# First stage of a hybrid decoder block: wide shift products, a tied TensorE order, later low parts, and the query banks emptied first

## Chip, core and metric

The kernel runs on one core of one Trainium2 chip. The metric is the device time of one execution in microseconds, as the median of several runs. The engines are TensorE (PE in the profile, its weight loads PEld), VectorE (DVE), ScalarE (ACT), GpSimd (POOL) and SyncE (SP, which issues loads).

## What is computed

One decoder layer on a sequence of 1024 positions with 1024 channels: a token-mixing part (a convolution branch and a stick-breaking attention branch, merged by gates) and a SwiGLU part, each between two RMS norms, with shift, scale and gate from a conditioning vector `c`. The change touches the start:

```python
c_act = jax.nn.silu(c)
mod = c_act @ ada_w[l] + ada_b[l]
sh1, sc1, ga1, sh2, sc2, ga2 = [m[:, None, :] for m in jnp.split(mod, 6, axis=-1)]
h = rmsnorm(x, pre_mix_g[l]) * (1.0 + sc1) + sh1
proj = h @ w_in        # gives GLU inputs, q, k, v and two merge gates
```

## The kernel before

Channels lie on the 128 partitions, so the 1024 channels are eight tiles (`KT` = 8, index k) of 128 x 1024; positions are the free dimension, in two halves of 512 (`NCH` = 2, index c). Products are made from float32r values split in two: a high part (`hhi`, `w0hi`) and a low part (`hlo`, `w0lo`, the rest). A product of h with a weight is three sums: high x high, low weight x high h, high weight x low h.

The first stage does this:

- Loads, all issued by SP (L98): `vec`, the eight tiles of `xT`, then the eight pieces of the modulation weight (`ada_w`, 1 MB each: shift half and scale half, in five buffers) with three weights (`w0raw`) between the first ones. These weights are those of the first query, the first key and the first GLU gate tile (`pq0`, `pk0`, `pgg0`, two PSUM banks each).
- The squares of x (ACT, L247) are summed over the channels on PE (L250) with a matrix of ones, and `rstd` is made from the sums (L327 to L338).
- For each k the scale is a dot product on DVE (`dots`, L121). The shift is, for k = 0 to 4, a product on PE (`shift_pe`, L280: eight one-column products, each two instructions, into column k of `psh`) and an addition on ACT (`shift_act`, L284); for k = 5 to 7 it is a second dot product on DVE.
- `x_op` (DVE, L296) multiplies x by scale and rstd in place; `hi_op` (ACT, L299) adds the shift and rounds to `hhi`; `lo_op` (DVE, L302) makes `hlo`. `w0_hi` (ACT, L307) and `w0_lo` (DVE, L311) split the three weights. POOL issues the stores of x (L101).
- `gemm_k` (L317) adds the k-th contribution to the three pairs of banks. Tile 0 is taken in halves; steps 0 and 1 serve the weights that are split by then.

Then `qk_pair(0)` empties the query banks (ACT L499 and L500, DVE L501 and L502) and the key banks (ACT L510 to L513, DVE L516), and `v_half(0)` makes the value tiles (L478): its two weights are loaded and split (`load_w`, L145 on ACT and L155 on DVE) into the slots that the first stage's weights had, its tiles go through the three banks of the pool `psm`, which the query and key banks held, and are evacuated by L482 (ACT) and L483 (DVE). Behind that come the GLU (`glu`), the attention (`attend`, z at L548 and L549) and everything else.

A planner writes the order of each engine's instructions when the kernel is built, from priorities and modelled durations. `pin` ties the instructions of the named engines to the order of the program. Before the change, DVE and ACT are tied in the first stage and PE is not; `qk_pair(0)` is not tied. The planner also adds the waits between engines.

Of the kernel before, what the change touches and what calls it, by code (L numbers as in the profile page):

```python
# [10 lines left out]
F32 = mybir.dt.float32  # L11
F32R = mybir.dt.float32r
AF = mybir.ActivationFunctionType
ALU = mybir.AluOpType
# [3 lines left out]
P = 128  # L18
D = 1024
T = 1024  # L20
KT = D // P
# [14 lines left out]
SH_DVE = (5, 6, 7)  # L36
# [24 lines left out]
C_ADAB = 32  # L61
# [8 lines left out]
def tile_block(ctx: ExitStack, tc: tile.TileContext, xT, vecs, ada1, ada2, win, wv, wcv, wat, wo, w1, w2, cvw, out):  # L70
    nc = tc.nc
    act, dve, pool, pe = nc.scalar, nc.vector, nc.gpsimd, nc.tensor
# [30 lines left out]
    vec = small.tile([P, NVEC], F32, name="vec")  # L103
# [4 lines left out]
    ones = small.tile([P, P], F32, name="ones")  # L108
# [60 lines left out]
    PINNED = tuple(getattr(mybir.EngineType, e) for e in ("PE", "DVE", "Activation"))  # L169
    START_PIN = PINNED[1:]  # L170

    def pin(start, engines=PINNED):
        last = {}
        for i in nc.cur_bb.bb.instructions[start:]:
            if i.engine not in engines:
                continue
            if i.engine in last:
                tc.add_manual_dep(i, last[i.engine].name,
                                  mybir.DependencyInfo(mybir.DependencyClass.NoSync, mybir.DependencyReason.SCHED_ONLY))
            last[i.engine] = i  # L180
# [16 lines left out]
    with ExitStack() as s0:  # L197
# [11 lines left out]
            load(aws[k], ada1[k])  # L209

        pvar = [ps0.tile([P, CH], F32, tag="pvar", name=f"pvar{c}", bufs=2) for c in range(NCH)]
        psh = ps0.tile([P, KT], F32, name="psh")
        rstd = p0.tile([P, T], F32, name="rstd0")
        csil = small.tile([P, KT], F32, name="csil")
        sc1 = small.tile([P, KT], F32, name="sc1")
# [36 lines left out]
        for k in range(KT - 1):  # L252
            if k == 0:
                square(0, rstd)
                continue
            sq = sq_tile0(f"sq{k}")
            square(k, sq)
            if k % 2:
                for c in range(NCH):
                    sums(sq, c, first=k == 1)  # L260
            elif k < KT - 2:
                dve.tensor_tensor(rstd, rstd, sq, op=ALU.add)
            else:
                for c in range(NCH):
                    dve.tensor_tensor(rstd[:, hs[c]], rstd[:, hs[c]], sq[:, hs[c]], op=ALU.add)
# [9 lines left out]
        def shift_of(k):  # L275
            return mod[:, k:k + 1]

        def shift_pe(k):
            for kt in range(KT):
                pe.matmul(psh[:, k:k + 1], aws[k][:, 0, kt * P:(kt + 1) * P], csil[:, kt:kt + 1],  # L280
                          start=(kt == 0), stop=(kt == KT - 1))

        def shift_act(k):
            act.activation(shift_of(k), psh[:, k:k + 1], AF.Identity, bias=vec[:, C_ADAB + k:C_ADAB + k + 1], scale=1.0)  # L284

        def dots(k):
            if k in SH_DVE:
# [10 lines left out]
        def hi_op(k, cols=slice(0, T)):  # L298
            act.activation(hhi[k][:, cols], xs[k][:, cols], AF.Identity, bias=shift_of(k), scale=1.0)  # L299
# [10 lines left out]
        def w0_lo(i):  # L310
            dve.tensor_tensor(w0s[i][1], w0raw[i], w0s[i][0], op=ALU.subtract)  # L311

        def gemm_k(b_, w, k):
            cols = slice(k * P, (k + 1) * P)
            for q, (st, mv) in enumerate(((0, 0), (0, 1), (1, 0))):
                for c, bank_ in b_.items():
                    pe.matmul(bank_, w[st][:, cols], h[mv][k][:, hs[c]], start=(k == 0 and q == 0),  # L317
                              stop=(k == KT - 1 and q == 2))

        for k in range(KT):  # L320
            hhi.append(hp.tile([P, T], F32R, tag="act", name=f"hhi{k}"))
            hlo.append(hp.tile([P, T], F32R, tag="act", name=f"hlo{k}"))

        shift_pe(0)
        for c in range(NCH):
            r, (m, a) = rstd[:, hs[c]], rt[c]
# [7 lines left out]
        for c in range(NCH):  # L334
            r, (m, a) = rstd[:, hs[c]], rt[c]
            dve.tensor_tensor(a, r, r, op=ALU.mult)
            dve.scalar_tensor_tensor(a, m, -0.5, a, op0=ALU.mult, op1=ALU.mult)
            dve.scalar_tensor_tensor(r, a, 1.5, r, op0=ALU.add, op1=ALU.mult)  # L338
            x_op(0, hs[c])
            hi_op(0, hs[c])  # L340
        dots(1)
        w0_lo(0)
        lo_op(0)
        for k in range(KT):
            kn = k + 1
            if kn < KT:
                if kn not in SH_DVE:
                    shift_act(kn)
                if kn + 1 < KT and kn + 1 not in SH_DVE:
                    shift_pe(kn + 1)  # L350
                x_op(kn)
                if kn <= 2:
                    w0_hi(kn)
                hi_op(kn)
                if kn + 1 < KT:
                    dots(kn + 1)
                if kn <= 2:
                    w0_lo(kn)
            if k:
                lo_op(k)  # L360
            store(xm_d[k], xs[k])
            ws = (q0b, k0b, gg0b)
            if k <= 1:
                for i in range(k + 1):
                    gemm_k(ws[i], w0s[i], k)
                for kk in range(k + 1):
                    gemm_k(ws[k + 1], w0s[k + 1], kk)
            else:
                for b_, w_ in zip(ws, w0s):
                    gemm_k(b_, w_, k)  # L370
        high.__exit__(None, None, None)
        pin(begin, START_PIN)
        sg0 = []
        for c in range(NCH):
            sg = sgp.tile([P, CH], F32, tag="sg", name=f"sg0_{c}", bufs=2)
# [29 lines left out]
    with ExitStack() as sC:  # L405
        pc = mkpool(sC, "pc")
        with ExitStack() as sA:
# [55 lines left out]
                                       scale=1.0)  # L463
                    load(u_d[ct][hf * (NG // 2):(hf + 1) * (NG // 2)].rearrange("g p m -> p g m"), o)

            def v_half(hf):
                w = [load_w(wv[hf, g], f"wv{hf}_{g}", act, pool if hf else dve) for g in range(2)]
                tiles = []
                for tb in range(KT):
                    if tb % 2 == 0:  # L470
                        vslot = pa.tile([P, 2, 4, 2, HD], F32R, tag="vst", name=f"vst{hf}_{tb}", bufs=4)
                    pv = bank(f"pv{hf}_{tb}")
                    tcols = slice(tb * P, (tb + 1) * P)
                    for k in range(KT):
                        whi, wlo = w[k // 4]
                        wc = slice((k % 4) * 256, (k % 4) * 256 + 256)
                        for i, (st, mv) in enumerate(((hhi, whi), (hlo, whi), (hhi, wlo))):
                            pe.matmul(pv[:, :256], st[k][:, tcols], mv[:, wc],  # L478
                                      start=(k == 0 and i == 0), stop=(k == KT - 1 and i == 2))
                    vt = vslot[:, tb % 2]  # L480
                    pvh = pv[:, :256].rearrange("p (h d) -> p h d", d=HD)
                    act.activation(vt[:, :, 0, :], pvh, AF.Copy)  # L482
                    dve.tensor_tensor(vt[:, :, 1, :], pvh, vt[:, :, 0, :], op=ALU.subtract)  # L483
                    tiles.append(vt)
                return tiles

            def qk_pair(p):
                qs = [pc.tile([P, T], F32R, tag="qst", name=f"qst{p}_{i}", bufs=3) for i in range(2)]
                ks = [pc.tile([P, T], F32R, tag="kst", name=f"kst{p}_{i}", bufs=3) for i in range(2)]
                kl = [pc.tile([P, T], F32R, tag="klo", name=f"klo{p}_{i}", bufs=3) for i in range(2)]  # L490
                A, B = slice(0, HD), slice(HD, P)
                if p == 0:
                    b = q0b
                else:
                    b = banks2(f"pq{p}")
                    gemm(b, load_w(win[8 + p], f"wq{p}"), h, range(KT))
                for c in range(NCH):
                    cs = slice(c * CH, (c + 1) * CH)
                    act.activation(qs[0][A, cs], b[c][A], AF.Copy)  # L499
                    act.activation(qs[1][B, cs], b[c][B], AF.Copy)  # L500
                    dve.tensor_tensor(qs[0][B, cs], b[c][A], qs[0][A, cs], op=ALU.subtract)  # L501
                    dve.tensor_tensor(qs[1][A, cs], b[c][B], qs[1][B, cs], op=ALU.subtract)  # L502
                if p == 0:
                    b = k0b
                else:
                    b = banks2(f"pk{p}")
                    gemm(b, load_w(win[12 + p], f"wk{p}"), h, range(KT))
                for c in range(NCH):
                    cs = slice(c * CH, (c + 1) * CH)
                    act.activation(ks[0][A, cs], b[c][A], AF.Copy)  # L510
                    act.activation(ks[1][B, cs], b[c][B], AF.Copy)
                    act.activation(ks[0][B, cs], b[c][A], AF.Copy)
                    act.activation(ks[1][A, cs], b[c][B], AF.Copy)  # L513
                    for i, src in enumerate((A, B)):
                        for dst in (A, B):
                            dve.tensor_tensor(kl[i][dst, cs], b[c][src], ks[i][src, cs], op=ALU.subtract)  # L516
                return qs, ks, kl
# [86 lines left out]
                return nxt  # L604

            with tc.high_priority(offset=SOONER):
                qk = qk_pair(0)
            v = v_half(0)
            for p in range(4):
                glu(p)  # L610
                if p == 2:
# [1223 lines left out]
```

## Time and profile before

| | us |
|---|---|
| median of 3 runs | 1400.02 (1399.16 to 1400.69) |
| profiled execution | 1400.8 |
| its span, first to last instruction | 1399.0 |
| first stage, up to the first value product | 68.1 |

The profile is one execution. A timeline row gives start, duration, engine, line, operation, output and inputs, tile and count; in brackets stands how long the engine was idle before and what ended that. Several instructions in one row have the duration from the first start to the last end. Matmuls are pipelined and their ends are modelled, so the pace of a sequence is read from the starts or from the chain of waits.

### The profile page before, as it was taken

Reading aid. Unit: us, or ns where it says so; the run is one execution under the profiler, and the core shown is the slowest. Engines: PE = TensorE matmul, PEld = TensorE weight load, DVE = VectorE, ACT = ScalarE, POOL = GpSimd, SP = SyncE. Lnnn points to the kernel's source line nnn. Section 1 sums busy time; section 2 is a strip of 40 time slices with the busy share of each in tenths; the row PEclk is TensorE's granted clock in tenths of the full one; section 3 lists DMA queues with packets and bytes.
Section 4 is the critical chain, followed back from the end, with each engine's and each line's share of the span. In section 5 each row is a group of like instructions: output and inputs, shape, how many; then the busy total and the mean of one; then the engine's idle time right before and its main releaser. Section 6 shows DMA issues by size and latency. Waiting matters only on the chain.

```text
span 1399.0 us, 18714 instructions
## 1 busy us (share of the span) xinstructions
PE 1370.6 (98%) x6778; PEld 1150.3 (82%) x6778; DVE 1043.6 (75%) x1592; ACT 651.5 (47%) x1147; POOL 109.4 (8%) x251
## 2 busy tenths in 40 slices
PE   8999999999999999999999999999999999999996
PEld 5898898998987887888887778888888887888886
DVE  7898586775858789677597887778887876785355
ACT  6375465464546456213366553334454444433441
POOL 0100000000000011000012100001111110000002
PEclk8999999999999999999999999999999999999999
DMA  9512050141359646855845635457777779586736
GB/s 384 204 31 76 31 166 31 61 121 46 123 191 318 203 128 233 308 183 176 311 136 188 196 115 192 142 179 249 252 241 263 248 240 398 176 330 229 249 110 121
DMA packets 94684, 265.01 MB, mean 189 GB/s; under 512 B 10048, under 2 KB 21440, under 8 KB 93568
## 3 DMA queue, kind: packets, MB, share of 16 engines
q1 hardware_dynamic: 74352, 201.68, 43.2%
q0 software_dynamic: 18224, 58.47, 11.9%
q10 hardware_dynamic: 2016, 3.67, 0.7%
q8 instruction: 53, 0.87, 0.3%
q14 instruction: 39, 0.32, 0.1%
HBM read 192.74 MB, written 71.04 MB: 189 GB/s over the span
## 4 chain that ended last, share of the span: by engine, by line
PE 76%; issue 14%; DVE 3%; DMA 3%; ACT 2%; POOL 1%; POOLq 0%; DVEq 0%; SPq 0%; ACTq 0%
PE ka L1001 14%; PE ka L1543 9%; PE kc L1001 8%; PE pwo L919 5%; PE pb L1543 4%; PE pgv L166 3%; PE pyc L747 3%; PE pya L166 3%; PE pv L478 3%; PE pq L166 2%; PE pk L166 2%; PE pgg L166 2%; PE pa L1543 2%; PE kb L1001 2%; PE tr L574 2%
## 5 line engine op out<-in xcount | busy, mean ns | idle before, releaser
L550 ACT ACTIVATE ka<-z 128x128 f32<-128x128 f32 (+2 forms) x96 | 47.4, 496 | 53.0 <-PE z L549 43.7
L556 DVE TENSOR_TENSOR_SCAN ka<-ka,eye 128x128 f32<-128x128 f32 (+1 forms) x64 | 51.9, 824 | 17.1 <-ACT ka L550 17.1
L1543 PE MATMUL ka<-gt,w2f 128*128 128x512 f32 x264 | 63.4, 389 | 0.0
L121 DVE SCALAR_TENSOR_TENSOR ada<-ada,cb 128x1024 f32<-128x1024 f32 x32 | 39.0, 1223 | 27.5 <-DMA ada<-in_ada_dram 27.5
L1543 PEld LDWEIGHTS ka<-gt,w2f 128*128 128x128 f32 x264 | 49.6, 188 | 10.3
L561 DVE TENSOR_TENSOR be<-be,ka 128x127 f32<-128x127 f32 (+2 forms) x96 | 52.0, 553 | 7.2 <-ACT be L552 1.8
L1109 PE MATMUL ke<-b,w_hi 128*128 128x512 f32 x176 | 55.2, 395 | 0.0
L552 ACT ACTIVATE be<-z 128x127 f32<-128x127 f32 (+2 forms) x96 | 47.0, 496 | 3.9 <-PE tr L574 3.8
L574 PE MATMUL tr<-ident,be 128*128 128x128 f32 x288 | 47.3, 272 | 0.0
L559 DVE TENSOR_TENSOR_SCAN ka<-ka 128x512 f32<-128x512 f32 x32 | 40.4, 1274 | 4.3 <-ACT ka L550 4.2
L458 PE MATMUL pcv<-ph,cvw 128*128 128x128 f32 x320 | 43.1, 274 | 0.0
L458 PEld LDWEIGHTS pcv<-ph,cvw 128*128 128x128 f32 x320 | 40.6, 191 | 0.7
L1109 PEld LDWEIGHTS ke<-b,w_hi 128*128 128x128 f32 x176 | 32.9, 188 | 7.9 <-issue 0.7
L580 ACT ACTIVATE ahi<-tr 128x512 fp32r<-128x512 f32 x48 | 28.3, 600 | 23.1 <-PE tr L574 17.4
L145 ACT ACTIVATE gt<-X 128x512 fp32r<-128x512 f32 x33 | 20.3, 629 | 39.6 <-DVE X L1586 17.5
L581 DVE TENSOR_TENSOR alo<-tr,ahi 128x512 fp32r<-128x512 f32 x48 | 32.3, 684 | 8.5 <-ACT ahi L580 8.3
L478 PE MATMUL pv<-wv_hi,hhi 128*128 128x256 f32 x128 | 36.7, 287 | 1.6 <-DVE vst L483 0.9
L145 ACT ACTIVATE s1o<-s 128x512 fp32r<-128x512 f32 x22 | 13.8, 629 | 50.4 <-PE ka L1001 44.0
L574 PEld LDWEIGHTS tr<-ident,be 128*128 128x128 f32 x288 | 34.8, 140 | 2.8
L402 PE MATMUL k<-hhi,a 128*128 128x512 f32 x112 | 35.4, 391 | 1.7 <-ACT ee L635 1.6
L478 PE MATMUL pv<-wv_hi,hlo 128*128 128x256 f32 x128 | 36.7, 287 | 0.0
L478 PE MATMUL pv<-wv_lo,hhi 128*128 128x256 f32 x128 | 36.3, 285 | 0.0
(550 smaller groups left out, 4178.6 us busy)
## 6 DMA issues: line engine op xcount, KB each, us to landing
w_d<-w2o POOLq DMA_DIRECT2D x44, 512.0 KB, 7.5
w2f<-w_d SPq DMA_DIRECT2D x44, 512.0 KB, 4.3
ada<-in_ada_dram SPq DMA_DIRECT2D x32, 512.0 KB, 5.1
w2r<-in_w_dram SPq DMA_DIRECT2D x44, 256.0 KB, 3.8
w1g<-in_w_dram SPq DMA_DIRECT2D x21, 512.0 KB, 3.7
w1u<-in_w_dram SPq DMA_DIRECT2D x21, 512.0 KB, 5.7
cvw<-in_cvw_dram SPq DMA_DIRECT2D x20, 512.0 KB, 3.7
ada_w<-in_ada_dram SPq DMA_DIRECT2D x8, 1024.0 KB, 14.0
```

The lines of the kernel that those rows point to most:

```text
L166: pe.matmul(bank, st[:, cols], mv[k][:, c * CH:(c + 1) * CH], start=(i == 0 and s == 0), stop=(i == n - 1 and s == 2))
L458: pe.matmul(cv[:, gi * TM:(gi + 1) * TM], wts[n][:, at:at + P], ph[:, g, SH - 1 - d:SH - 1 - d + TM], start=(d == 0), stop=(d == SH - 1))
L478: pe.matmul(pv[:, :256], st[k][:, tcols], mv[:, wc], start=(k == 0 and i == 0), stop=(k == KT - 1 and i == 2))
L550: act.activation(kap[:, s_lo:s_hi], z[:, zo:zo + w], AF.Sigmoid, bias=0.0, scale=-0.125)
L552: act.activation(beta[:, :m], z[:, zo:zo + m], AF.Sigmoid, bias=0.0, scale=0.125)
L556: dve.tensor_tensor_scan(rev, rev, eye[:, CH - w:][:, ::-1], 0.0, op0=ALU.mult, op1=ALU.add)
L561: dve.tensor_tensor(beta[:, :m], beta[:, :m], kap[:, s_lo + 1:s_lo + 1 + m], op=ALU.mult)
L574: pe.transpose(tr[:, o:o + P], probs[ii][:, jo:jo + P], ident)
L919: pe.matmul(bank_, st[:, cols], mv[k][:, cs], start=(k == 0 and q == 0), stop=(k == KT - 1 and q == 2))
L1001: pe.matmul(bank_, st[:, cols], t[:, mv], start=(first and j == 0 and s == 0), stop=(j == HK - 1 and s == 2), skip_group_check=not first)
L1109: pe.matmul(kbs[f], wes[f][st][:, cols], t[:, mv], start=(i == 0 and j == 0 and q == 0), stop=(j == HK - 1 and q == 2), skip_group_check=i ...
L1543: pe.matmul(dst, w[st][:, cols], g[mv], start=first and s == 0, stop=last and s == 2, skip_group_check=more)
```

## The change

The scalars of `c` are copied over 128 equal columns (`csb`, made by DVE in the middle of the squares), and a shift is a product with 128 moving columns into one of four slots of `psh`, of which ACT reads the first column. `shift_pe` for tile 2 goes between the two halves of tile 0, and the later ones stand one step further ahead. `gemm_k` becomes `gemm_q`, which takes the list of part products (HH, HL, LH: weight part, then h part): a step makes HH and LH of its own tile and HL of the tile before, and the last step makes both HL, one weight after the other. PE is tied to the program's order from the first shift to the end of the stage. `qk_pair` takes a function that it calls after each query half; for the first pair this loads and splits a value weight, and DVE and ACT are tied there.

```diff
-    def pin(start, engines=PINNED):
+    def pin(start, engines=PINNED, end=None):
         last = {}
-        for i in nc.cur_bb.bb.instructions[start:]:
+        for i in nc.cur_bb.bb.instructions[start:end]:
...
-        psh = ps0.tile([P, KT], F32, name="psh")
+        psh = ps0.tile([P, 4, P], F32, name="psh")
+        csb = p0.tile([P, KT, P], F32, name="csb")
...
             elif k < KT - 2:
                 dve.tensor_tensor(rstd, rstd, sq, op=ALU.add)
+                if k == 2:
+                    for kt in range(KT):
+                        dve.tensor_scalar(csb[:, kt], ones, csil[:, kt:kt + 1], None, op0=ALU.mult)
...
         def shift_pe(k):
             for kt in range(KT):
-                pe.matmul(psh[:, k:k + 1], aws[k][:, 0, kt * P:(kt + 1) * P], csil[:, kt:kt + 1],
+                pe.matmul(psh[:, k % 4], aws[k][:, 0, kt * P:(kt + 1) * P], csb[:, kt],
                           start=(kt == 0), stop=(kt == KT - 1))
 
         def shift_act(k):
-            act.activation(shift_of(k), psh[:, k:k + 1], AF.Identity, bias=vec[:, C_ADAB + k:C_ADAB + k + 1], scale=1.0)
+            act.activation(shift_of(k), psh[:, k % 4, 0:1], AF.Identity, bias=vec[:, C_ADAB + k:C_ADAB + k + 1], scale=1.0)
...
-        def gemm_k(b_, w, k):
+        def gemm_q(b_, w, k, *sms, cs=(0, 1)):
             cols = slice(k * P, (k + 1) * P)
-            for q, (st, mv) in enumerate(((0, 0), (0, 1), (1, 0))):
-                for c, bank_ in b_.items():
-                    pe.matmul(bank_, w[st][:, cols], h[mv][k][:, hs[c]], start=(k == 0 and q == 0),
-                              stop=(k == KT - 1 and q == 2))
+            for st, mv in sms:
+                for c in cs:
+                    pe.matmul(b_[c], w[st][:, cols], h[mv][k][:, hs[c]], start=(k == 0 and st == 0 and mv == 0),
+                              stop=(k == KT - 1 and mv == 1))
+
+        HH, HL, LH = (0, 0), (0, 1), (1, 0)
...
+        pe_begin = len(nc.cur_bb.bb.instructions)
         shift_pe(0)
...
             x_op(0, hs[c])
             hi_op(0, hs[c])
+            gemm_q(q0b, w0s[0], 0, HH, cs=(c,))
+            if c == 0:
+                shift_pe(2)
...
-                if kn + 1 < KT and kn + 1 not in SH_DVE:
-                    shift_pe(kn + 1)
+                if kn + 2 < KT and kn + 2 not in SH_DVE:
+                    shift_pe(kn + 2)
...
-            ws = (q0b, k0b, gg0b)
-            if k <= 1:
-                for i in range(k + 1):
-                    gemm_k(ws[i], w0s[i], k)
-                for kk in range(k + 1):
-                    gemm_k(ws[k + 1], w0s[k + 1], kk)
+            ws = list(zip((q0b, k0b, gg0b), w0s))
+            if k == 0:
+                gemm_q(*ws[0], 0, LH, HL)
+                gemm_q(*ws[1], 0, HH, HL)
+            elif k == 1:
+                gemm_q(*ws[0], 1, HH, LH)
+                gemm_q(*ws[1], 0, LH)
+                gemm_q(*ws[1], 1, HH, LH)
+                gemm_q(*ws[2], 0, HH, HL)
+                gemm_q(*ws[2], 1, HH)
             else:
-                for b_, w_ in zip(ws, w0s):
-                    gemm_k(b_, w_, k)
+                for i, bw in enumerate(ws):
+                    if k == 2 and i == 2:
+                        gemm_q(*bw, 0, LH)
+                        gemm_q(*bw, 1, LH)
+                    gemm_q(*bw, k, HH, LH)
+                    if k == KT - 1:
+                        gemm_q(*bw, k - 1, HL)
+                        gemm_q(*bw, k, HL)
+                if k < KT - 1:
+                    for bw in ws:
+                        gemm_q(*bw, k - 1, HL)
         high.__exit__(None, None, None)
         pin(begin, START_PIN)
+        pin(pe_begin, PINNED[:1])
...
-            def v_half(hf):
-                w = [load_w(wv[hf, g], f"wv{hf}_{g}", act, pool if hf else dve) for g in range(2)]
+            def v_half(hf, w=None):
+                if w is None:
+                    w = [load_w(wv[hf, g], f"wv{hf}_{g}", act, pool if hf else dve) for g in range(2)]
...
+                    if between:
+                        between(c)
...
             with tc.high_priority(offset=SOONER):
-                qk = qk_pair(0)
-            v = v_half(0)
+                begin = len(nc.cur_bb.bb.instructions)
+                wv0 = []
+                qk = qk_pair(0, lambda c: wv0.append(load_w(wv[0, c], f"wv0_{c}", act, dve)))
+                pin(begin, START_PIN)
+            v = v_half(0, wv0)
```

More of the change, by code (lines that the diff above doesn't have):

```diff
@@ L485, in v_half, with qk_pair @@
                 return tiles
-            def qk_pair(p):
+            def qk_pair(p, between=None):
                 qs = [pc.tile([P, T], F32R, tag="qst", name=f"qst{p}_{i}", bufs=3) for i in range(2)]
```

## The prediction

> **What bounds the kernel now.** The page's head and busy shares come first: the end is set by TensorE (PE).
>
> ```profile
> span 1399.0 us, 18714 instructions
> ...
> PE 1370.6 (98%) x6778; PEld 1150.3 (82%) x6778; DVE 1043.6 (75%) x1592; ACT 651.5 (47%) x1147; POOL 109.4 (8%) x251
> ```
>
> Next come the views by windows, since the change touches the first 80 us only (columns: window, its length, busy time and count for PE, PEld, DVE, ACT and POOL, then granted clock, DMA share, GB/s).
>
> ```profile
> 16.87:20.28 3.41, 3.41 (x21) 2.44 (x19) 3.23 (x6) 2.53 (x4) 0.00 (x0) 1.00 1.01 416
> ...
> 23.00:24.00 1.00, 0.00 (x0) 0.00 (x0) 0.96 (x2) 0.00 (x0) 0.00 (x0) 0.85 0.90 365
> ...
> 33.00:34.00 1.00, 1.00 (x6) 0.91 (x5) 0.96 (x3) 1.00 (x1) 0.53 (x1) 0.53 0.95 393
> ...
> 36.00:67.00 31.00, 31.00 (x146) 25.84 (x145) 24.83 (x36) 8.77 (x10) 4.61 (x17) 1.00 0.49 200
> ...
> 67.00:79.00 12.00, 10.37 (x82) 9.70 (x81) 11.22 (x17) 11.43 (x21) 0.00 (x0) 1.00 0.30 88
> ...
> 79.00:200.00 121.00, 120.95 (x757) 108.26 (x756) 96.34 (x144) 67.92 (x145) 2.70 (x27) 1.00 0.21 66
> ```
>
> The granted clock falls from 1.0 to 0.5 in the window from 23 us (0.85 as a mean puts the fall near 23.7) and comes back near 33.9: 10.2 us at half speed. From 36 us on PE has no gap until 67, then loses 1.63 us of 12, then runs full. So what the stage loses, it loses before 34 and between 67 and 79. The PE timeline shows the first place:
>
> ```profile
> 17.65 1.02 PE L250 MATMUL pvar<-sq,ones 128*128 128x512 f32 x2
> ...
> 18.51 1.84 PE L280 MATMUL psh<-csil,ada_w 128*128 128x1 f32 x16
> ...
> 20.71 1.93 PE L280 MATMUL psh<-csil,ada_w 128*128 128x1 f32 x16 [0.36 <-ACT mod L284]
> ...
> 24.95 0.79 PE L317 MATMUL pq<-hhi,w0hi 128*128 128x512 f32 x1 [1.97 <-ACT hhi L299]
> ...
> 25.54 3.41 PE L280 MATMUL psh<-csil,ada_w 128*128 128x1 f32 x16
> ```
>
> Up to 18.5 PE is full with wide products (the sums). Two shift columns (one-column products), a single wide product and a gap of 1.97 us follow, and in them the clock falls; the third shift column then takes 3.41 us. The chain of waits gives the wide product's two rates:
>
> ```profile
> 30.01 1.71 PE pq L317 x4
> ...
> 60.54 0.91 PE pq L317 x4
> ```
>
> That is 0.43 us each at half clock and 0.2275 at full. The end of the stage, from the timelines:
>
> ```profile
> 64.21 1.06 ACT L145 ACTIVATE wv_hi<-wv_raw 128x1024 fp32r<-128x1024 f32 x1 [6.12 <-PE pq L317]
> ...
> 66.73 0.61 PE L317 MATMUL pgg<-hhi,w0lo 128*128 128x512 f32 x2
> ...
> 68.11 0.36 PE L478 MATMUL pv<-wv_hi,hhi 128*128 128x256 f32 x1 [0.77 <-DVE qst L502]
> ...
> 78.53 0.39 PE L478 MATMUL pv<-wv_hi,hhi 128*128 128x256 f32 x1 [0.86 <-DVE vst L483]
> ```
>
> The query products are done at 64.21 (the value weights wait for their slot), the gate products, 12 more, at 64.21 + 12 x 0.2275 = 66.95; the first value product waits for DVE to empty the query bank, the fourth value tile for DVE to evacuate the first.
>
> **The change part by part.** *Wider shift columns.* Each shift is 16 instructions still, with 128 moving columns in place of one. The trace has that shape and type in the convolution, and DVE has the shape of the new 128-column copies of the scalars:
>
> ```profile
> L458 PE MATMUL pcv<-ph,cvw 128*128 128x128 f32 x320 | 43.1, 274 | 0.0
> ...
> 3.22 1.66 DVE L240 TENSOR_SCALAR dia<-ident,csil 128x128 f32<-128x128 f32 x8
> ...
> 11.64 1.23 DVE L262 TENSOR_TENSOR rstd<-rstd,sq 128x1024 f32<-128x1024 f32 x1 [1.39 <-ACT sq L247]
> ...
> 14.22 1.29 DVE L265 TENSOR_TENSOR rstd<-rstd,sq 128x512 f32<-128x512 f32 x2 [1.35 <-ACT sq L247]
> ```
>
> 43.1/320 = 0.135 us, so 2.16 us a shift against 1.84 to 1.93. The bounds are 1.84 (columns cost nothing) and 3.41 (the dearest shift above); I take 2.16, from the same shape at full clock. Five shifts cost PE 1.4 us more. The eight copies cost DVE 1.66 us and stand ahead of the L262 of 11.64: 1.39 lies in its idle time, 0.27 moves it, and the next DVE instruction, which idles 1.35, swallows that. Without this cover it would be 1.66 on DVE.
>
> *TensorE's order tied, low parts a step behind.* PE now runs in program order, each shift further ahead, so it waits for the shift weights' loads. Their issue and time to landing (the DMA view, one issue to an answer; the fourth and fifth lie in the row of four, the fifth at 14.3):
>
> ```profile
> 10.49 0.33 SPq L98 DMA_DIRECT2D ada_w<-in_ada_dram  x1
> ...
> 13.05 12.64 SPq L98 DMA_DIRECT2D ada_w<-in_ada_dram  x4
> ...
> ada_w<-in_ada_dram SPq DMA_DIRECT2D x1, 1024.0 KB, 13.9
> ...
> ada_w<-in_ada_dram SPq DMA_DIRECT2D x1, 1024.0 KB, 15.1
> ...
> ada_w<-in_ada_dram SPq DMA_DIRECT2D x1, 1024.0 KB, 17.2
> ```
>
> They land at 24.4, 28.15 and 31.5. PE then goes: shift 0 from 18.51 to 20.8; ACT's 0.3 us; shift 1 to 23.3; first query product to 23.5; wait to 24.4; shift 2 to 26.6; second product to 26.8; wait to 28.15; shift 3 to 30.3. Behind each waiting shift stand PE's own products. Of the others, ACT's addition for shift 1 may wait until shift 2 is done at 26.6, as all shifts lie in one PSUM tile; behind it on ACT stands the key weight's high part, then done by 28, and DVE takes that at 30.38 (below). The load that reuses shift 0's buffer is issued 0.4 later, behind loads queued up to 31.5. Eight wide products (4 query, 4 key) take 1.8, to 32.1; shift 4 (landed) 2.2, to 34.3. There remain 16, 22 and 4 x 18 products for steps 1 to 6, and 24 for step 7, the query's 8 first. At 0.2275 the query group ends 118 products on: 34.3 + 26.8 = **61.1**, where it now ends at 64.21. Gate products end 16 later, at 64.8, against 66.95 now. This takes full clock throughout: no PE gap is over 1.4 us, and in every stretch of 3.4 us some 60% holds products of 128 columns or more.
>
> Nothing they need is late: DVE and ACT keep their order.
>
> ```profile
> 26.59 1.28 DVE L302 SCALAR_TENSOR_TENSOR hlo<-x,mod,hhi 128x1024 fp32r<-128x1024 f32 x1
> ...
> 30.38 1.22 DVE L311 TENSOR_TENSOR w0lo<-w0raw,w0hi 128x1024 fp32r<-128x1024 f32 x1
> ...
> 56.81 2.59 DVE L302 SCALAR_TENSOR_TENSOR hlo<-x,mod,hhi 128x1024 fp32r<-128x1024 f32 x2
> ...
> 56.93 1.16 ACT L299 ACTIVATE hhi<-x,mod 128x1024 fp32r<-128x1024 f32 x1 [3.98 <-DVE x L296]
> ```
>
> The first low part is there at 27.9 and used after 30.3; the last high part at 58.1 and the last low part at 59.4, used from 59.3 and 60.6 on. The last two leave at most 1.2 us for a faster PE: what is late next is DVE.
>
> The clock is the term to weigh. [...]
>
> *Query evacuation ahead.* ACT and DVE do the same pieces, the first query half before the first value weight.
>
> ```profile
> 65.17 0.57 ACT L499 ACTIVATE qst<-pq 64x512 fp32r<-64x512 f32 x1
> ...
> 66.56 0.68 DVE L501 TENSOR_TENSOR qst<-pq,qst 64x512 fp32r<-64x512 f32 x1
> ...
> 71.14 5.62 DVE L516 TENSOR_TENSOR klo<-pk,kst 64x512 fp32r<-64x512 f32 x8 [0.50 <-ACT kst L513]
> ...
> 76.80 1.23 DVE L155 TENSOR_TENSOR wgv_lo<-wgv_raw,wgv_hi 128x1024 fp32r<-128x1024 f32 x1
> ...
> 78.05 1.09 DVE L483 TENSOR_TENSOR vst<-pv,vst 128x256 fp32r<-128x256 f32 x3
> ```
>
> After the query products: two ACT halves of 0.6 and two DVE parts of 0.7 free the first bank at 61.1 + 2.7 = 63.8, a microsecond before PE asks for it at 64.8. The 0.77 goes. But the chain behind it is as long as before: ACT's two weights, four query and four key pieces still stand ahead of the key's low parts, 71.14 - 64.21 = 6.9 after the query group, so these start at 68.0, and first value tile's DVE part at 68.0 + 5.6 + 1.3 = 75.0 instead of 78.05. PE has 9.9 us of work there (66.95 to 78.53, less 1.63 idle) and 10.7 us to do it in, so DVE's chain decides. The split of the second value weight comes at 67.7, up to 1.2 us after PE's fifth block wants it; that wait fits in the slack.
>
> **The sum:** 64.21 - 61.1 = 3.1, taken as **3.0 us** for semaphore time, carried to 78.5 and, as PE is full from 79 us on, to the end. If DVE's part came sooner, the gain would be 2.15 (gate products) + 1.63 (idle) = 3.8, and 5.0 with PE at its limit of 59.4. At 3.41 a shift, shift 1 would end at 25.6, shifts 2, 3 and 4 at 29.2, 32.9 and 38.1: 3.8 later than above, 0.7 us slower than now. The profiled execution took 1400.8 us, 1.8 outside its span, and would take 1397.8; it lies 0.8 over the median of 1400.02, within the runs' spread, so by the median **1397.0 us**.
>
> **The rivals.** *The clock still falls.* It fell once after a gap of 1.97 us; two gaps of 0.9 and 1.35 remain. Half speed from 23.7 to 33.9 would make shifts 2 and 3 some 4.3 us each: they would end at 28.7 and 33.4, the eight products at 35.3, the query group 3.2 later than above, at 64.3: 1400.1, no gain. Against it: from 16.9 to 20.3 the clock held 1.0 with wide products up to 18.5 alone, half of that time. [...] Chance 0.12. It covers also the case that the wider columns do not do what they are for.
>
> *The order of the rest is written anew, and worse.* Only the first stage is tied. The planner interleaves attention with value and gate products by its own modelled times, and an earlier start can reshuffle them. Its price is in the waits that exist:
>
> ```profile
> 400.00:560.00 160.00, 155.44 (x681) 126.06 (x681) 126.84 (x193) 87.42 (x143) 11.93 (x22) 1.00 0.66 220
> ...
> PE pyc L747 <- ACT wc_hi L145: 2.1, 1, 2.1
> ```
>
> 4.6 us idle in 160, the longest wait 2.1. To end slower than before by 2.8 the new order must lose 5.8, more than this idle time again: 1402.8 or more, and it decides against the change from 3.0 on. For it: such waits hang on which product the planner puts first. Against: 79 to 200 us has 0.05 us idle. Chance 0.08; giving back 1 to 3 us, 0.10, about 1399.
>
> *The same, better:* a wait of 2 us goes as well, 1395. Chance 0.10.
>
> **How the numbers follow.** The forecast, a gain of 1.5 to 4.5, has 0.60: 1395.5 to 1398.5. The measurement can tell about 0.2%, 2.8 us, from no change, so the 3.0 sits on the border: of the 0.60 I put 0.37 beyond it. Faster: 0.37 + 0.10 = 0.47. Same: 0.23 + 0.12 + 0.10 = 0.45. Slower: 0.08. The range leaves out the worst and the best tenth: 1393.8 to 1400.8.
>
> **What would show it.** Right: clock 1.0 through 20 to 40 us; shifts of some 2.2 us; PE waiting for loads at 23.5 and 26.8 and for nothing until about 64.8; query group done near 61; no wait of the first value product; fourth value tile near 75.5. Wrong: clock at 0.5 past 24; a shift over 2.5 us; loads landing later than 31.5; or all of this as said and the span shorter by less, with new waits after 79 us.

## The result, and the profile after

| | median us | lowest to highest | runs |
|---|---|---|---|
| before | 1400.39 | 1398.91 to 1405.85 | 22 |
| changed | 1397.39 | 1395.85 to 1399.34 | 22 |

The ratio is 0.9975, with a 95% interval of 0.9968 to 0.9983: 3.0 us faster. Three of the 22 executions before lie near 1405; a likely reason is given below. In the batches that follow, one execution each of before, a2_cols32, c1_old_evac and z2_f1 took 1966 us or more, and these are left out of every median and ratio. The profiled execution of the changed kernel took 1397.39 us. Its page begins:

```profile
span 1395.6 us, 18715 instructions
...
PE 1367.1 (98%) x6778; PEld 1146.5 (82%) x6778; DVE 1046.8 (75%) x1600; ACT 652.2 (47%) x1147; POOL 109.3 (8%) x251
```

TensorE still sets the end. The span is 3.4 us shorter, and TensorE is busy for 3.5 us less. The windows of the changed kernel, with the columns of the prediction's (the last but two is the granted clock):

```profile
23.00:24.00 1.00, 0.67 (x5) 0.35 (x4) 0.93 (x3) 0.00 (x0) 0.00 (x0) 1.00 0.98 397
...
33.00:34.00 1.00, 1.00 (x11) 1.00 (x11) 1.00 (x2) 0.55 (x1) 0.35 (x1) 1.00 0.92 385
...
67.00:79.00 12.00, 11.62 (x91) 10.90 (x90) 10.82 (x19) 10.03 (x21) 0.00 (x0) 1.00 0.36 115
...
79.00:200.00 121.00, 121.00 (x756) 108.11 (x755) 98.39 (x146) 70.31 (x150) 2.87 (x29) 1.00 0.20 65
...
400.00:560.00 160.00, 155.30 (x677) 125.67 (x676) 125.63 (x191) 87.28 (x139) 11.96 (x23) 1.00 0.64 223
```

The clock stays at 1.0 where it was 0.85 and 0.53. Between 33 and 34 us PE does 11 products where it did 6. Between 67 and 79 it idles 0.38 us instead of 1.63. The later windows are as full as they were. The PE timeline of the changed kernel shows the shifts:

```profile
19.08 1.95 PE L284 MATMUL psh<-csb,ada_w 128*128 128x128 f32 x16
...
24.95 2.05 PE L284 MATMUL psh<-csb,ada_w 128*128 128x128 f32 x16 [1.28 <-DMA ada_w<-in_ada_dram]
26.76 0.47 PE L321 MATMUL pq<-hhi,w0hi 128*128 128x512 f32 x1
28.79 2.02 PE L284 MATMUL psh<-csb,ada_w 128*128 128x128 f32 x16 [1.55 <-DMA ada_w<-in_ada_dram]
...
63.76 1.07 PE L321 MATMUL pgg<-hlo,w0hi 128*128 128x512 f32 x4
64.67 0.28 PE L503 MATMUL pv<-wv_hi,hhi 128*128 128x256 f32 x1
```

PE waits for loads before shifts 2 and 3, 2.8 us in all. The first value product follows the last gate product with no wait. The end of the stage on ACT and DVE:

```profile
61.01 0.59 ACT L524 ACTIVATE qst<-pq 64x512 fp32r<-64x512 f32 x1 [2.37 <-PE pq L321]
...
68.08 5.62 DVE L543 TENSOR_TENSOR klo<-pk,kst 64x512 fp32r<-64x512 f32 x8 [0.48 <-ACT kst L540]
...
75.11 0.76 DVE L508 TENSOR_TENSOR vst<-pv,vst 128x256 fp32r<-128x256 f32 x2
```

The query group ends at 61.01 (before: 64.21), and the first value tile's DVE part begins at 75.11 (before: 78.05). That lead of 2.94 us is carried to the end, where the span is 3.4 us shorter.

### The profile page after: what moved, and what is told of

Same layout as the page of the kernel before. It is cut to its first block, busy times and chain, and to the rows that moved or that the text cites. A ratio compares the mean times of both kernels' runs of the same rounds, so it can differ in the third digit from the quotient of the medians.

```text
span 1395.6 us, 18715 instructions
## 1 busy us (share of the span) xinstructions
PE 1367.1 (98%) x6778; PEld 1146.5 (82%) x6778; DVE 1046.8 (75%) x1600; ACT 652.2 (47%) x1147; POOL 109.3 (8%) x251
## 4 chain that ended last, share of the span: by engine, by line
PE 77%; issue 14%; DMA 3%; DVE 2%; ACT 2%; POOL 1%; SPq 0%; POOLq 0%; DVEq 0%; ACTq 0%
PE ka L1031 15%; PE ka L1573 9%; PE kc L1031 8%; PE pwo L949 6%; PE pb L1573 4%; PE pgv L166 3%; PE pyc L777 3%; PE pya L166 3%; PE pv L503 3%; PE pgg L166 2%; PE pk L166 2%; PE pq L166 2%; PE pa L1573 2%; PE kb L1031 2%; PE tr L601 2%
## 5 line engine op out<-in xcount | busy, mean ns | idle before, releaser
L1573 PE MATMUL ka<-gt,w2f 128*128 128x512 f32 x264 | 63.4, 389 | 0.0
## 6 DMA issues: line engine op xcount, KB each, us to landing
ada_w<-in_ada_dram SPq DMA_DIRECT2D x8, 1024.0 KB, 13.7
```

The source lines that it names most:

```text
L1573: pe.matmul(dst, w[st][:, cols], g[mv], start=first and s == 0, stop=last and s == 2, skip_group_check=more)
```

## The experiments

The first shift starts at a slightly different time in each execution (18.16 to 19.08 us), so the time from its start to the end of the query group is compared: 45.70 us before (64.21 - 18.51), 41.93 after (61.01 - 19.08). In the profiled execution of each kernel:

| kernel | ratio to before, 95% interval | shift 0 to query group, us | us at half clock, without the last 10 us of the span |
|---|---|---|---|
| before | 1 | 45.70 | 10.2 |
| changed | 0.9975, 0.9968 to 0.9983 | 41.93 | 0 |
| a1_narrow | 1.0012, 0.9999 to 1.0026 | 49.55 | 20.5 |
| a2b_cols32 | 1.0011, 0.9999 to 1.0023 | 45.91 | 13.7 |
| a3_fill | 1.0021, 1.0007 to 1.0035 | 46.95 | 6.8 |
| b1_wide_only | 0.9998, 0.9986 to 1.0009 | 45.96 | 3.4, and 3.4 at 555 us |
| d1_untied | 0.9992, 0.9981 to 1.0004 | 44.28 | 3.4, from 67.16 us on |
| e1_lo_in_step | 1.0004, 0.9993 to 1.0015 | 47.04 | 3.4 |
| c1_old_evac | 0.9982, 0.9972 to 0.9993 | 41.97 | 0 |
| f1_loads | 0.9954, 0.9938 to 0.9969 | 41.64 | 0 |
| z2_f1 (the same again) | 0.9977, 0.9968 to 0.9986 | 41.80 | 0 |
| z1_after (the change again) | 0.9976, 0.9966 to 0.9986 | 41.91 | 0 |

Each ratio is to executions of before on the same chip as that kernel. The theory was that of the prediction: wide columns hold the clock, and the early end of the query group that this gives is carried on. The rivals were that the order alone does it, and that the evacuation's order brings a good part.

### One-column shifts in the new order

```diff
-pe.matmul(psh[:, k % 4], aws[k][...], csb[:, kt],
+pe.matmul(psh[:, k % 4, 0:1], aws[k][...], csil[:, kt:kt + 1],
```

> The changed kernel with one thing put back: the shift products move one column again instead of 128; the tied order, the low parts a step behind and the early query evacuation stay. Theory (the clock goes by how dense the products are, so the width is what holds it): the granted clock falls to 0.5 near 24 us and comes back near 34; shifts 2 and 3 take some 3.4 us each, the query group ends near 63.5 instead of 61.0, and 2.5 of the 3.4 us in the span are lost: ratio to before near 0.9995. Rival (the order holds the clock, since it has no gap as long as the 1.97 us of before): clock 1.0 throughout, query group done at 61.0 or sooner, ratio near 0.9975.

The median is 1404.61 us. Windows of this kernel, then its PE timeline:

```profile
23.00:24.00 1.00, 0.00 (x0) 0.00 (x0) 0.96 (x3) 0.00 (x0) 0.00 (x0) 0.82 0.98 397
...
44.00:45.00 1.00, 1.00 (x5) 0.77 (x5) 1.00 (x2) 0.00 (x0) 0.00 (x0) 0.94 1.05 426
```

```profile
24.25 3.57 PE L284 MATMUL psh<-csil,ada_w 128*128 128x1 f32 x16 [1.38 <-DMA ada_w<-in_ada_dram]
```

The means of 0.82 and 0.94 put the fall at 23.64 and the return at 44.12. The clock was expected to be low for as long as before; it was low for twice as long, and the query group, expected 2.5 us later than with the change, came 7.6 us later. That is the usual case but not every one: eight of its twelve executions took 1404.4 to 1407.1 us at a mean clock of 0.988 to 0.990, four 1399.6 to 1401.3 at 0.992 to 0.993. With narrow shifts the new order holds the clock no better than the old one, and as a whole it is no faster. So the order alone is not the gain.

### 32 columns

```diff
-pe.matmul(psh[:, k % 4], aws[k][...], csb[:, kt],
+pe.matmul(psh[:, k % 4, 0:32], aws[k][...], csb[:, kt, 0:32],
```

> The changed kernel with shift products of 32 columns instead of 128. [...]

The only profile of this run is that of the execution which is left out, with a mean clock of 0.556. The ratio of the other nine was 0.9985 (0.9973 to 0.9997), at mean clocks of 0.992 to 0.994. So it ran once more:

> The 32-column shifts a second time, for a profile with the clock of an undisturbed execution. [...] Rival (32 columns are enough): clock 1.0, query group at 41.9.

```profile
23.00:24.00 1.00, 0.29 (x1) 0.00 (x0) 0.96 (x2) 0.00 (x0) 0.00 (x0) 0.52 0.98 397
...
36.00:37.00 1.00, 1.00 (x8) 1.00 (x7) 1.00 (x2) 0.00 (x0) 0.00 (x0) 0.65 1.01 397
```

These are windows of a2b_cols32: half clock from 23.04 to 36.70. The two ratios differ, and the second median is 1402.54. The first ratio's interval still overlaps that of 128 columns, so the times alone do not decide; the clock does. All nineteen executions have a mean clock of 0.989 to 0.994, as before has, and none comes near the 0.996 to 0.998 of the change. So 32 columns did not hold the clock here. For a2b_cols32 a query group at 43.5 us or later had been forecast; it came at 45.91.

### Narrow shifts with useless wide products beside them

Six wide float32 products, of two instructions each, whose result is overwritten are added to a1_narrow.

```diff
+        def fill(n):
+            for _ in range(n):
+                pe.matmul(gg0b[0], ones, xs[KT - 1][:, hs[0]], start=True, stop=True)
...
             gemm_q(q0b, w0s[0], 0, HH, cs=(c,))
+            fill(2)
...
                 gemm_q(*ws[1], 0, HH, HL)
+                fill(2)
```

> One-column shifts in the tied order, as in the run with narrow shifts, with six wide float32 products of no use (two after each of the two first query products and two behind step 0, written to the gate bank before it is used, 0.86 us each at full clock). [...]

Windows, then PE rows of a3_fill:

```profile
21.00:22.00 1.00, 1.00 (x9) 1.00 (x10) 0.96 (x2) 1.00 (x2) 0.00 (x0) 0.82 1.08 446
...
28.00:29.00 1.00, 1.00 (x8) 1.00 (x9) 1.00 (x1) 0.00 (x0) 0.00 (x0) 0.77 0.98 401
```

```profile
24.12 3.62 PE L289 MATMUL pgg<-x,ones 128*128 128x512 f32 x4
...
31.71 1.84 PE L284 MATMUL psh<-csil,ada_w 128*128 128x1 f32 x16
...
37.05 1.84 PE L284 MATMUL psh<-csil,ada_w 128*128 128x1 f32 x16
```

The author's forecast for this kernel, clock 1.0 and a query group at 43 to 44.5 us, was missed; it came at 46.95. The clock had fallen at 21.64, before the first two fillers (the four instructions at 24.12) ran at half speed. But it came back at 28.46, after 6.8 us where a1_narrow had 20.5, and then held 1.0 through narrow shifts at 31.71 and 37.05 (1.84 us each). So in this run a narrow shift among wide products did not by itself bring the clock down. What held it there was not shown. As a whole the kernel is slower than before, so the fillers are no substitute.

### 128 columns in the old order

This is the kernel before, with the tiles, copies and wide shift product of the change and nothing else of it.

> The kernel before with the 128 equal columns alone; the order, the low parts and the query evacuation are those of before. Theory: the clock stays at 1.0, the third shift takes some 1.9 us instead of 3.4, but PE then waits for hhi1 (30.3), the gate weight's low part (35.3) and hlo1 (36.5) in its old order, so that step 2 starts near 41.0 instead of 42.5 and the query group ends near 62.7: ratio near 0.9989. Rival (the order, not the width, holds the clock): the clock falls as before, query group at 64.2 or later, ratio 1.000 to 1.001.

PE rows and windows of this kernel (the windows cut at the fall and the return):

```profile
24.85 0.50 PE L321 MATMUL pq<-hhi,w0hi 128*128 128x512 f32 x1 [1.85 <-ACT hhi L303]
...
66.22 0.61 PE L321 MATMUL pgg<-hhi,w0lo 128*128 128x512 f32 x2
68.29 0.35 PE L482 MATMUL pv<-wv_hi,hhi 128*128 128x256 f32 x1 [1.45 <-DVE qst L506]
```

```profile
22.83:26.24 3.41, 1.56 (x12) 1.38 (x12) 3.34 (x6) 1.81 (x3) 0.72 (x1) 1.00 1.03 420
26.24:29.66 3.42, 3.42 (x14) 3.03 (x13) 3.42 (x4) 0.60 (x1) 0.38 (x1) 0.50 1.00 416
```

The expected 0.9989 and query group at 62.7 were missed; there is no gain. In the first stage the clock is at half for one stretch of 3.42 us instead of 10.2. Of those 10.2 PE waited 1.26 anyway (23.69 to 24.95), so this should give (10.2 - 1.26 - 3.4)/2 = 2.8 us, an estimate. Most of it comes back as waits. The waits view of this kernel (in total, times, longest):

```profile
PE pq L321 <- DVE hlo L306: 1.5, 2, 0.7
```

PE waits 1.5 us for low parts, which the same view of before does not name at all, and 1.45 for the emptied query bank where that was 0.77. The last gate products start only 0.51 us sooner than before (66.22, 66.73). The 0.8 us that remain of the 2.8 are not accounted for. So a faster clock alone mostly makes PE early for DVE; the other half of the change is needed to use it.

### The order not tied

```diff
-        pin(pe_begin, PINNED[:1])
```

> The changed kernel without the tie of PE's order in the first stage; the program's order of the products stays. Theory (the program's new order does the work, and the planner follows it nearly): query group within 0.5 us of 61.0, clock 1.0, ratio 0.9970 to 0.9980. Rival (the tie is needed, the planner moves products ahead of the shifts and opens a gap): clock falls again or query group over 62, ratio 0.9985 or more.

PE and ACT timeline rows, then windows, of this kernel:

```profile
24.68 0.50 PE L322 MATMUL pq<-hhi,w0hi 128*128 128x512 f32 x1 [1.86 <-ACT hhi L304]
...
62.09 0.62 PE L322 MATMUL pq<-hlo,w0hi 128*128 128x512 f32 x2
...
62.99 0.61 PE L322 MATMUL pgg<-hlo,w0hi 128*128 128x512 f32 x2
65.31 0.35 PE L503 MATMUL pv<-wv_hi,hhi 128*128 128x256 f32 x1 [1.70 <-DVE qst L527]
...
62.51 0.59 ACT L524 ACTIVATE qst<-pq 64x512 fp32r<-64x512 f32 x1 [4.69 <-PE pq L322]
```

```profile
67.00:68.00 1.00, 1.00 (x7) 1.00 (x7) 0.95 (x3) 0.96 (x3) 0.00 (x0) 0.58 0.86 98
...
70.00:71.00 1.00, 1.00 (x8) 1.00 (x8) 0.97 (x3) 0.98 (x3) 0.00 (x0) 0.71 0.96 197
```

The clock holds 1.0 through the first stage here, with a gap of 1.86 us. But the query group, expected as early as with the change, comes 2.35 us later: the planner leaves the query's last low-part products almost to the end, at 62.09. From shift 0 on, all gate products are done no later than in the changed kernel (63.4 - 18.23 = 45.2 against 64.67 - 19.08 = 45.6), and yet PE waits 1.70 us for the query bank, and the clock falls behind that, for 67.16 to 70.58. So the tie's worth is in the last step, where the query's products go first, as well as in the first.

### Low parts in their own step

```diff
-                gemm_q(*ws[0], 1, HH, LH)
+                gemm_q(*ws[0], 1, HH, HL, LH)
...
-                    gemm_q(*bw, k, HH, LH)
+                    gemm_q(*bw, k, HH, LH, HL)
```

Key and gate in step 1 likewise; the lines that make HL of the tile before are gone.

> The changed kernel with the low parts in their own step again (high x high, then the two low products, weight by weight); wide shifts, tied order and early evacuation stay. Theory (in the tied order the step behind is what keeps PE from waiting for DVE): PE waits some 2.4 us for hlo1 in step 1, and the query group, with all 122 products behind that, ends 45.1 us after the first shift starts instead of 41.9; ratio to before 0.9990 to 1.0000, a microsecond or two worse still if the clock falls in the new gap. Rival (the low parts' place does not matter, PE is full anyway): query group 42 to 43 after the first shift, ratio 0.9970 to 0.9980.

Timeline and windows of this kernel:

```profile
36.29 0.73 PE L321 MATMUL pq<-hlo,w0hi 128*128 128x512 f32 x2 [2.26 <-DVE hlo L306]
```

```profile
34.19:37.60 3.41, 1.31 (x6) 1.09 (x7) 3.41 (x4) 0.07 (x1) 0.00 (x0) 1.00 1.01 408
37.60:41.01 3.41, 3.41 (x10) 2.65 (x9) 3.37 (x5) 1.22 (x2) 0.53 (x1) 0.50 1.04 428
```

As expected: PE waits 2.26 us for the low part of tile 1, the clock falls for one stretch behind it (1.7 us), and the query group is later by 5.1 us. The wait and the clock are 4.0 of that. All of the gain is gone. The step's delay of the low parts is a part that the change cannot do without.

### The old evacuation

```diff
-                begin = len(nc.cur_bb.bb.instructions)
-                wv0 = []
-                qk = qk_pair(0, lambda c: wv0.append(load_w(...)))
-                pin(begin, START_PIN)
-            v = v_half(0, wv0)
+                qk = qk_pair(0)
+            v = v_half(0)
```

> The changed kernel with the query evacuation and the value weights' splits as before (weights first, nothing tied there). Theory (the chain behind the query group is as long either way, so this edit brings at most the first wait): query group done at 61.0 as in the changed kernel, first value product some 0.2 to 0.6 us later than 64.7, fourth value tile near 75.9 as in the changed kernel, ratio to before 0.9973 to 0.9980. Rival (the early evacuation brings a third of the gain or more): fourth value tile a microsecond or more later, ratio 0.9983 or more. The planner's order behind this stage is written anew, which may move either by some tenths.

ACT and DVE rows of this kernel's timeline:

```profile
68.65 1.04 ACT L145 ACTIVATE wv_hi<-wv_raw 128x1024 fp32r<-128x1024 f32 x1
...
72.01 1.23 DVE L155 TENSOR_TENSOR wv_lo<-wv_raw,wv_hi 128x1024 fp32r<-128x1024 f32 x1
...
76.36 0.42 DVE L508 TENSOR_TENSOR vst<-pv,vst 128x256 fp32r<-128x256 f32 x1 [0.55 <-ACT vst L507]
```

The query group ends as early as with the change (41.97), yet the first value tile's DVE part starts at 76.36, 15.98 us behind it; before it was 13.84 (78.05 - 64.21), after 14.10 (75.11 - 61.01). So the forecast that the edit brings at most the first wait was missed. Left free, the planner now takes all query pieces ahead of the first value weight's low part and puts the second value weight's split behind the key pieces. The waits view of this kernel shows PE waiting for the first weight's low part (`wv_lo`) and, longer, for the key's:

```profile
PE pv L503 <- DVE klo L543: 0.9, 1, 0.9
...
PE pv L503 <- DVE wv_lo L155: 0.7, 1, 0.7
```

By the traces this edit brings 1.9 us at that point. By the times (median 1399.28, ratio in the table) the two intervals overlap, so the traces show it and the times only lean that way. The edit takes away the tie and the new place of the splits together; which of the two brings it was not separated.

### Loads asked for sooner

The third weight is loaded one piece of `ada_w` later, and the last two shifts stand nearer to the landing of their loads.

```diff
-W0_AT = (0, 1, 2)
+W0_AT = (0, 1, 3)
...
-                if kn + 2 < KT and kn + 2 not in SH_DVE:
-                    shift_pe(kn + 2)
+                if k == 0:
+                    shift_pe(3)
...
                 gemm_q(*ws[1], 0, LH)
+                shift_pe(4)
```

> The changed kernel with the third first-stage weight loaded one place later, so that the fourth shift weight lands some 1.25 us sooner, and shift 4 put behind the first six products of step 1. Theory (PE's wait for that load is real, but DVE's last high and low parts, at 39.6 and 40.9 us after the first shift in the changed kernel, bound the end): PE's waits for shift weights fall from 2.8 to some 1.5 us, the query group ends 41.3 to 41.6 after the first shift instead of 41.9, ratio 0.9968 to 0.9980. Rival (PE alone is the bound): query group at 40.7, ratio near 0.9965.

```profile
26.58 2.02 PE L284 MATMUL psh<-csb,ada_w 128*128 128x128 f32 x16 [0.28 <-DMA ada_w<-in_ada_dram]
...
59.80 0.59 ACT L525 ACTIVATE qst<-pq 64x512 fp32r<-64x512 f32 x1 [2.06 <-PE pq L321]
```

Of the shift rows in this kernel's timeline, the one above waits 0.28 us where the changed kernel's last wait was 1.55. All such waits, in the waits view of this kernel:

```profile
PE psh L284 <- DMA ada_w<-in_ada_dram: 2.0, 3, 1.3
```

That is 0.8 us less, and the query group comes 0.3 us sooner. The ratio of six runs was more than that can give. So it ran again beside the change itself:

> The changed kernel itself, beside the version with the later third weight on the same chip. Theory (the later weight only takes 0.3 us out of the stage, since DVE bounds it): ratio to before 0.9968 to 0.9980, and within 0.0008 of the other version's. Rival (that version is faster by 2 us or more, as its first comparison may be read): ratios apart by 0.0014 or more.

> The version with the third first-stage weight one place later and shift 4 inside step 1, a second time. Theory: query group 41.6 us after the first shift, first value tile's DVE part some 55.8 after it against 56.0 in the changed kernel, ratio 0.9965 to 0.9978. Rival: 0.9960 or less.

The change has 1397.42 us, this kernel 1397.47: no difference. Of the 0.8 us less waiting, 0.1 to 0.3 arrives at the query group (41.80 and 41.64 against 41.91 and 41.93); where the rest goes was not followed. A part of what made the six runs fast is the mean clock: one of them was at 0.996 and five at 0.997 or 0.998, where the second time five of ten were at 0.996. The rest stays open; the two series ran on different chips.

### What the mean clock of every execution adds

Each run lists its mean granted clock. The executions of before that ran beside these kernels, 89 in all, have 0.994 (25 of them, 1398.4 to 1401.7 us) down to 0.989 (14, all 1404.2 to 1406.6). A drop of 0.005 over 1400 us is 7 us of full clock lost, 14 us more at half speed; the medians of the two groups are 5.6 us apart. So the 1405s are, by this estimate, executions in which the clock stayed down longer or fell once more. b1_wide_only has 0.995 to 0.997 and 1400.8: the better clock without the time. Even its four executions at 0.997 took 1398.9 to 1400.5 us.

The change has 0.998 in nine of its 22 (1395.85 to 1397.39), 0.997 in six, and 0.996 in seven (1397.59 to 1398.98). In its profiled execution, one of those at 0.998, the clock is at half only at the end, where PE has nothing to do:

```profile
1388.66:1395.60 6.94, 0.00 (x0) 0.00 (x0) 3.39 (x10) 0.00 (x0) 0.00 (x0) 0.50 0.45 151
```

Half of 6.94 us over the span is 0.0025, all that the 0.998 lacks. At 0.996 the clock must have been low for about 0.002 x 1397 x 2 = 5.6 us more, 2.8 to 8.4 by the rounding of the means, an estimate. One more stretch of 3.4 us, as in the profile of b1_wide_only, lies in that, and at half clock it would cost 1.7 us; the medians of the two groups, 1396.59 and 1398.35, are 1.8 us apart. Where that stretch lies in the changed kernel no trace shows. The profile of b1_wide_only shows that it need not be the first stage. PE's row and the windows there, then the row of the same wait in the changed kernel:

```profile
555.40 0.79 PE L751 MATMUL pyc<-hhi,wc_hi 128*128 128x512 f32 x1 [2.13 <-ACT wc_hi L145]
...
551.90:555.31 3.41, 1.38 (x7) 0.80 (x5) 3.23 (x5) 2.06 (x4) 0.50 (x1) 1.00 1.02 418
555.31:558.73 3.42, 3.33 (x8) 2.65 (x9) 2.23 (x3) 0.56 (x2) 0.54 (x1) 0.50 1.03 419
```

```profile
553.22 0.50 PE L777 MATMUL pyc<-hhi,wc_hi 128*128 128x512 f32 x1 [2.12 <-ACT wc_hi L145]
```

At the end of a wait of 2.13 us for a later weight the clock of b1_wide_only fell for one stretch of 3.42 us; in the profiled execution of the change it held 1.0 through the same wait of 2.12 us (the window 400:560 above has 1.00). That wait also stood in the kernel before (2.1 us).

## Why the prediction held, point by point

- **The clock held, as forecast, but on less than the prediction said.** "Some 60%" wide work in every stretch of 3.4 us was too much. By the rows of after, PE has nothing from 26.76 + 0.23 to 28.79, so the worst such stretch has 1.61 of 3.41 us, 47%, and a wait of 1.55 us stands where "no PE gap is over 1.4 us" was said. The shift was shorter than taken and the waits longer, and both made it thinner. That such a plan keeps full clock was the author's estimate, and no run shows which share or which gap decides. What the runs show is 1.0 through the first stage of the changed kernel, and in b1_wide_only a fall at 26.24, with 41% in the 3.41 us before (last section). Whether the clock of the first stage, as in the first rival, fell in an execution that was not profiled stays open. The seven executions at 0.996 have more half clock than the others, but it may lie elsewhere, as b1_wide_only shows.
- **The shift's price was mis-sized.** Taken at 2.16 us from the convolution's shape, it is 1.81 (24.95 to 26.76), as if the columns cost nothing, which was the lower bound. Five shifts: 1.75 us too dear.
- **The waits for loads were mis-sized the other way.** 0.9 and 1.35 forecast, 1.28 and 1.55 measured: 0.58 us more. z1_after has the same sum, 2.8, so it is no accident of one execution. The loads themselves came as forecast: shift 2 starts 5.87 us after shift 0 and shift 3 9.71, where 5.89 and 9.64 were worked out. PE was at the loads sooner because its shifts were shorter, so this error and the one above are two sides of one. f1_loads and its repetition show that removing part of the waits gives nothing that the times can tell.
- **The query group**, forecast at 61.1, ends at 61.01. Shift 0 started 0.57 later than assumed, so the way there was about 0.7 shorter than worked out. The last wait for a load stands ahead of shift 3, so only shifts 3 and 4 count there, at 0.35 less each. That the two figures agree within 0.1 is luck of the later start.
- **The evacuation was under-read.** "ACT and DVE do the same pieces" and a chain of 6.9 us held for the tied order: 68.08 - 61.01 = 7.07. But the prediction gave the edit only the 0.77 us wait, as if the old order would have stayed. c1_old_evac shows that it would not: behind the faster stage the planner writes another, 1.9 us worse. The total came out right because the sum followed the tied order.
- **The tie** was weighed by the clock and the loads. The sum did put the query's products first in the last step, but named no price for that. d1_untied shows one: without the tie its last low-part products come near the end, the query group is 2.35 us later, and PE waits 1.70 us for the query bank.
- **The rest stayed**: 79 to 200 us is full and 400 to 560 has 4.70 us idle where it had 4.56. The second rival did not come. The gain of 3.0 was of the right size, and near the border of what can be told, as said.

No single part that was tried alone carries it (the intervals are in the table). Width alone gives 0.9998, the new order with one column 1.0012, the change without its tie 0.9992, without the step's delay 1.0004. Together they give 0.9975.

## What to carry to other kernels

Look at the granted clock beside the busy share: in before, PE was busy for all of the microsecond from 33 to 34, at a granted clock of 0.53, and did 6 products where the changed kernel did 11 at 1.00. Try wider columns for small products: here 128 took 1.81 us a shift where one took 1.80, and with the new order they went with a clock of 1.0. A faster first stage paid here only as far as the engines behind it were ordered for it (c1_old_evac lost 1.9 us there): trace what is late next, and tie that order too where a planner would write it anew. Compare the mean clock of single executions before a time is believed; six runs gave 0.9954 for a kernel whose next ten gave 0.9977, with more executions at the lower clock among the ten.

## What was not expected of the hardware

**Every stretch at half clock that was measured between the start and the last 10 us is close to a whole multiple of 3.41 us**: 3.41 (e1_lo_in_step), 3.42 (d1_untied, and twice in b1_wide_only), 6.82 (a3_fill), 13.66 (a2b_cols32), 20.48 (a1_narrow, 44.12 - 23.64), and 10.2 in before. Why was not shown.

**Gaps of about 2 us stood before falls, and gaps as long passed without one.** The clock fell behind gaps of 1.85 (b1_wide_only) and 2.26 us (e1_lo_in_step). It held behind 1.86 us in d1_untied, and through 2.12 us at 553 us in the changed kernel. So in these runs the length of the gap alone does not tell it. Nor does the share of a stretch that holds wide products. By the starts, the 3.41 us before the fall had 38% in e1_lo_in_step (36.29 to 37.60 of 34.19 to 37.60) and 41% in b1_wide_only (24.85 to 26.24 of 22.83 to 26.24). The clock held with 48% in before (16.87 to 20.28, wide until 18.51) and with 45% in d1_untied (22.79 to 26.20, wide from 24.68 on). But in the changed kernel a stretch of 3.41 us around the gap of 2.12 has at most 1.29 us of products, 38%, and the clock held there too. No run varied the share alone.

**A float32 product of 128 columns cost here what one column cost**, each with a weight of its own: 1.81 us from the start of a shift to the next product (24.95 to 26.76) against 1.80 for the narrow one before (20.71 to 22.51), 16 instructions each. The row of before in which the narrow one ends:

```profile
22.51 0.47 PE L317 MATMUL pq<-hhi,w0hi 128*128 128x512 f32 x1
```
